# A two-layer decoder trunk in split fp32 on one core: the down projection in rounds of six, six, six and four hidden tiles, and the token factors stored as (rounded, rest) columns side by side

## The chip, the cores and the metric

The kernel runs on one core of a Trainium2 chip. The metric is device time of one execution in microseconds, as the median of three runs.

## The reference, cut to what matters

512 tokens of width 1024 go through a gated short convolution layer with a SwiGLU feed-forward stage, and then through a sliding-window attention layer with another one. All is float32. The change touches the two feed-forward stages alone:

```python
D_MODEL, SEQ = 1024, 512
D_FF = 2816

def swiglu(h, w_gate_up, w_down):
    g, u = jnp.split(h @ w_gate_up, 2, axis=-1)
    return (jax.nn.silu(g) * u) @ w_down

for l in range(2):
    ...  # conv or attention, with residual
    ff = swiglu(rmsnorm(h, ffn_pre_norm[l]), ffn_w_gate_up[l], ffn_w_down[l])
    h = h + rmsnorm(ff, ffn_post_norm[l])
```

## The kernel before

**Numbers.** Every float32 operand is split into a rounded part (`hi`, type fp32r) and the rest (`lo = x - hi`). A product is three TensorE matmuls, rounded by rest, rounded by rounded and rest by rounded (`mm3`, L191 to L193). ScalarE makes `hi` with a copy (L469 for the weights), VectorE subtracts for `lo` (L470).

**Hidden tiles.** The hidden width 2816 is 22 tiles of 128. The first two (`PLAIN`) are computed plainly. The other 20 go in ten *pairs*, q = 0 to 9. A pair's gate and up products are one 2 by 2 block matrix product, done with seven block products in place of eight: p = 1, 2, 6, 5, 7, 3, 4 in this order, one *job* each (`gate_jobs`). Products 1, 6, 7, 4 accumulate in one chain of PSUM banks, X (tile `gx`), products 5 and 3 in Z (`gz`), product 2 in Y (`gy`).

**Token factors.** Products 4 to 7 need sums and differences of token blocks. `factors()` makes them once per layer, in eight tiles `xt` of 128 by 1024. Such a tile holds two blocks of 256 columns: first the rounded columns of both, then the rests of both. For the products 6, 7 and 4 one matmul reads rounded and rest together as its moving operand (L1048, `two[:, :, c : c + 256]`, 2 by 256 columns, 512 apart in the tile) into 512 columns of PSUM, and a second multiplies the weight's rest with the 256 rounded columns (L1050). A pair has 3 x 8 such twos, a layer 240, the kernel 480.

**Down rounds.** The down projection is done in rounds over the hidden tiles that are ready, `ROUNDS`, again with seven block products, whose sum ends in SBUF tiles `mix`: after each product VectorE adds its two PSUM banks to `mix` (L639; in a layer's first round ScalarE makes eight of the fourteen by a copy, L637). A round of four tiles has 7 jobs with 1024 columns of weights each. A round of six has 11 (`order` in `down_jobs`): three hold the last third of two products, and there the next product of a chain follows its predecessor after six matmuls of another chain, and not after twelve. The last four hidden tiles have no such round: they are multiplied plainly in `close`, with four *closing* weights.

**The line.** All jobs of a layer stand in one line (`in_line`). With G for a pair's seven jobs and D for a down round's, the line is

```
G0 G1 G2 D0 G3 G4 D1 G5 G6 D2 G7 G8 G9 D3
```

Weights are fetched on SyncE's queue (L440) into seven buffers `raw`, split three jobs ahead of their use (`LINE_LEAD`), and used by TensorE. When a pair is done, the parts of making the down round's activations (`pair_sums`) are spread, one behind each job that follows; the first five jobs of an 11-job round take none (`alone`). The closing weights' splits stand in the line at `LAST`, 9, 7, 5 and 3 jobs from its end.

**Sums of weights in DRAM.** The block products need sums of weight blocks. They are made by GpSimd's DMA queue in DRAM (tiles `hsum`, L538), as plain copies and then accumulating transfers, in two or four steps (`Sums`). `BEGIN` says at which point of the program a block's steps begin: `0p1` is the end of pair 1 in layer 0, `0s1` the end of down round 1, `a3` a stage of the attention; `g09` are the sums for pair 9 of layer 0, `d02` for its down round 2. Each later point issues the next step, paced behind the splits.

Of the kernel before, what the change touches and what calls it, by code (L numbers as in the profile page):

```python
# [18 lines left out]
S = 512  # L19
KT = D // P  # L20
F = 2816
NF = F // P
ROUNDS = [(0, 6), (6, 10), (10, 14), (14, 18), (18, 22)]

PLAIN = 2

# [1 line left out]

BEGIN = {
# [4 lines left out]
}  # L34


# [36 lines left out]
def yoco_kernel(  # L73
# [45 lines left out]
    def wide(s, dt=F32):  # L119
        return wides.tile([P, D], dt, tag="wide", name=name(s))  # L120
# [118 lines left out]
    class Update:  # L239
# [124 lines left out]
        def factors(self):  # L364


            x = self.x[0]
            made = {p: [] for p in range(1, 8)}
            for p, k0, c in ((1, 0, 0), (2, 4, 0), (3, 4, 256)):
                made[p] = [[a[:, c : c + 256] for a in x[k0 + k]] for k in range(4)]  # L370
            for j in range(2):
                q11, q21, q12, q22 = (self.parts[i, hf, j] for hf in range(2) for i in range(2))

                nc.vector.tensor_tensor(out=q11, in0=q11, in1=q12, op=ALU.subtract)
                nc.vector.tensor_tensor(out=q12, in0=q22, in1=q12, op=ALU.subtract)
                nc.vector.scalar_tensor_tensor(out=q22, in0=q22, scalar=-1.0, in1=q11,
                                               op0=ALU.mult, op1=ALU.subtract)
                nc.vector.scalar_tensor_tensor(out=q21, in0=q22, scalar=-1.0, in1=q21,
                                               op0=ALU.mult, op1=ALU.subtract)
                for p, q in ((6, q22), (5, q11), (7, q12), (4, q21)):  # L380
                    two = wide("xt", F32R)
                    hi, lo = two[:, :S], two[:, S:]
                    two = two.rearrange("p (i c) -> p i c", i=2)
                    nc.scalar.activation(hi, q, AF.Copy)
                    nc.vector.tensor_tensor(out=lo, in0=q, in1=hi.bitcast(F32),
                                            op=ALU.subtract)
                    made[p] += [[hi[:, c : c + 256], lo[:, c : c + 256], two[:, :, c : c + 256]]
                                for c in (0, 256)]
            return made

    class Ahead:
# [156 lines left out]
    for l in range(2):  # L548
        for q in range((NF - PLAIN) // 2):
            sums_of[f"g{l}{q}"] = Sums([w_gb[l, q, b] for b in (2, 3, 0, 1)], [P, D],  # L550
                                        q not in ADDED)
        for rd, (f0, f1) in enumerate(ROUNDS[:-1]):
            k = slice(f0 // 2, f1 // 2)
# [401 lines left out]
    def ffn(l, before, ahead, gain, gpres, following):  # L955
# [5 lines left out]
        def gate_pair(pg, pu):  # L961
# [12 lines left out]
            return pair_sums(gr, acts[0])  # L974

        def gate_jobs(q, factors, out, to, then):


# [130 lines left out]

        acts = [[] for _ in ROUNDS]  # L1110
        mix = [None] * NB
        pss = [bank("pgu", ps_mm) for _ in range(4)]
        with tc.manual_schedule(engines=ALL):
# [29 lines left out]
            jobs, behind_one = [], []  # L1143
            for rd, (f0, f1) in enumerate(ROUNDS):
                last = rd == len(ROUNDS) - 1
                for f in range(max(f0, PLAIN), f1, 2):
                    q = (f - PLAIN) // 2
                    jobs += gate_jobs(q, factors, pair_acts if last else pair_sums, acts[rd],
                                      lambda q=q: sum_on(f"{l}p{q}"))
                    if behind_one and not (last and f < f1 - 2):  # L1150
                        jobs += behind_one.pop()
                if last:
                    break
                down = down_jobs(range(f0 // 2, f1 // 2), acts[rd], rd == 0,
                                 sums_of[f"d{l}{rd}"],
                                 lambda rd=rd: sum_on(f"{l}s{rd}"))
                behind_one.append(down)
# [260 lines left out]
    with tc.manual_schedule(engines=ALL):  # L1418
        last_tile(res, [[(0, 4)], [(0, 5)], [], [(0, 6), (0, 7), (1, 0), (1, 1)],
                        [(1, f) for f in (4, 5, 2, 3, 6, 7)]])  # L1420
        for hf in range(2):
            c = slice(hf * 256, (hf + 1) * 256)
# [194 lines left out]
```

## Time and profile before

| | |
|---|---|
| runs | 1026.5, 1026.7, 1026.81 us; median 1026.7 |
| the profiled execution | 1026.46 us, of which the span of instructions 1024.7 us |
| granted TensorE clock | 0.999 |
| DMA | 244.52 MB, mean 239 GB/s |

The profile is of one execution. "Busy" TensorE time is drawn with modelled ends: a matmul's row lasts longer than the distance to the next one's start, since they overlap. Where durations and starts differ, the starts tell the rate. Layer 0's feed-forward stage lies at about 188 to 500 us of the span, layer 1's at 693 to 1018 us.

### The profile page before, as it was taken

The page shows a single profiled execution, that of the slowest core. Times are in us where ns is not written, and L with a number is a line of the kernel's source. Part 1 is how long each engine was busy: PE and PEld are TensorE (multiplying, and loading weights), DVE is VectorE, ACT ScalarE, POOL GpSimd, SP SyncE. Part 2 cuts the span into 40 slices and gives each one's busy share as a digit, 9 for nine tenths or more (in the row PEclk, how much of TensorE's full clock was granted, in tenths as well). Part 3 has the DMA queues.
Part 4 walks back from the last instruction along what each step waited for, and adds up shares of the span by engine and source line. Part 5 has one row for each costly group of instructions (what it writes and reads, how often), then busy time and mean ns, then how long its engine had stood idle before and what let it go on. Part 6 is the DMA issues. An engine that isn't in the chain of part 4 may idle for free.

```text
span 1024.7 us, 16538 instructions
## 1 busy us (share of the span) xinstructions
PE 1015.1 (99%) x6168; PEld 900.3 (88%) x6168; DVE 858.7 (84%) x1440; ACT 582.3 (57%) x1035; POOL 196.9 (19%) x259
## 2 busy tenths in 40 slices
PE   9999999999999999999999999999999999999997
PEld 8888888999889898998897888889998998989986
DVE  5766767889789988989869998778997898889896
ACT  7323445865655454666476776677666554645641
POOL 0443033112111111000123653232111010110001
PEclk9999999999999999999999999999999999999999
DMA  9897689459979699879504779976899576998742
GB/s 357 288 266 225 184 255 350 136 167 292 348 238 296 195 305 307 267 210 318 170 5 160 187 229 277 254 264 153 270 289 328 167 245 226 299 298 249 240 149 82
DMA packets 66576, 244.52 MB, mean 239 GB/s; under 512 B 7872, under 2 KB 8384, under 8 KB 54720
## 3 DMA queue, kind: packets, MB, share of 16 engines
q1 hardware_dynamic: 51328, 145.98, 38.9%
q0 software_dynamic: 14592, 96.48, 36.9%
q8 instruction: 48, 0.79, 0.3%
q10 hardware_dynamic: 576, 1.02, 0.3%
q14 instruction: 32, 0.26, 0.1%
HBM read 237.15 MB, written 102.76 MB: 332 GB/s over the span
## 4 chain that ended last, share of the span: by engine, by line
PE 85%; DVE 8%; ACT 2%; DMA 2%; issue 2%; POOL 0%; DVEq 0%; ACTq 0%
PE gx L1048 10%; PE gx L1050 5%; PE pcub L191 4%; PE pcub L192 4%; PE pcub L193 4%; PE gz L193 3%; PE gz L192 3%; PE gz L191 3%; PE px L191 3%; PE px L193 3%; PE px L192 3%; PE pmix L191 2%; PE pmix L192 2%; PE pmix L193 2%; DMA raw<-in_w_gb_dram 2%; PE gy L193 2%
## 5 line engine op out<-in xcount | busy, mean ns | idle before, releaser
L470 DVE TENSOR_TENSOR wlo<-raw,whi 128x1024 fp32r<-128x1024 f32 x225 | 274.8, 1227 | 64.5 <-ACT whi L469 64.1
L469 ACT ACTIVATE whi<-raw 128x1024 fp32r<-128x1024 f32 x225 | 234.0, 1051 | 104.8 <-DVE raw L457 22.3
L1048 PE MATMUL gx<-xt,whi 128*128 128x512 f32 x480 | 172.5, 399 | 0.1
L1050 PE MATMUL gx<-xt,wlo 128*128 128x256 f32 x480 | 135.0, 281 | 0.0
L1048 PEld LDWEIGHTS gx<-xt,whi 128*128 128x128 f32 x480 | 90.4, 188 | 19.7 <-DVE st L1008 0.3
L538 POOL DMA_DIRECT2D hsum<-in_w_gb_dram x96 | 63.7, 751 | 143.9 <-ACT whi L469 82.6
L1050 PEld LDWEIGHTS gx<-xt,wlo 128*128 128x128 f32 x480 | 90.9, 189 | 0.1
L1024 ACT ACTIVATE st<-gx 128x256 f32<-128x256 f32 x120 | 43.0, 379 | 63.1 <-PE gx L1050 47.8
L538 POOL DMA_DIRECT2D hsum<-hsum x32 | 25.3, 790 | 258.9 <-ACT whi L469 192.0
L1008 DVE TENSOR_TENSOR st<-gx,st 128x256 f32<-128x256 f32 x160 | 62.9, 420 | 4.3 <-ACT st L1024 2.9
L192 PE MATMUL pcub<-xhi,whi 128*128 128x512 f32 x168 | 65.4, 389 | 0.0
L191 PE MATMUL pcub<-xlo,whi 128*128 128x512 f32 x168 | 65.4, 389 | 0.0
L193 PE MATMUL pcub<-xhi,wlo 128*128 128x512 f32 x168 | 65.4, 389 | 0.0
L1062 ACT ACTIVATE gr<-gr 128x1024 f32<-128x1024 f32 x20 | 21.3, 1065 | 49.2 <-DVE gr L1008 49.2
L191 PE MATMUL px<-wlo,ahi 128*128 128x512 f32 x120 | 46.8, 390 | 0.1
L192 PE MATMUL px<-whi,ahi 128*128 128x512 f32 x120 | 46.7, 389 | 0.0
L193 PE MATMUL px<-whi,alo 128*128 128x512 f32 x120 | 46.7, 389 | 0.0
L193 PE MATMUL gz<-xhi,wlo 128*128 128x256 f32 x160 | 45.4, 284 | 0.0
L191 PE MATMUL gy<-xlo,whi 128*128 128x256 f32 x160 | 45.3, 283 | 0.0
L192 PE MATMUL gy<-xhi,whi 128*128 128x256 f32 x160 | 45.3, 283 | 0.0
L193 PE MATMUL gy<-xhi,wlo 128*128 128x256 f32 x160 | 45.3, 283 | 0.0
L192 PE MATMUL gx<-xhi,whi 128*128 128x256 f32 x160 | 45.3, 283 | 0.0
(265 smaller groups left out, 3064.5 us busy)
## 6 DMA issues: line engine op xcount, KB each, us to landing
hsum<-in_w_gb_dram POOLq DMA_DIRECT2D x96, 512.0 KB, 7.9
raw<-hsum SPq DMA_DIRECT2D x88, 512.0 KB, 7.6
raw<-in_w_gb_dram SPq DMA_DIRECT2D x60, 512.0 KB, 7.6
hsum<-in_w_dn_dram POOLq DMA_DIRECT2D x36, 512.0 KB, 8.8
raw<-in_w_dn_dram SPq DMA_DIRECT2D x32, 512.0 KB, 6.0
hsum<-hsum POOLq DMA_DIRECT2D x28, 512.0 KB, 5.9
raw<-in_w_in_dram SPq DMA_DIRECT2D x21, 512.0 KB, 7.8
hsum<-in_w_dn_dram POOLq DMA_DIRECT2D x12, 768.0 KB, 12.8
```

The lines of the kernel that those rows point to most:

```text
L191: nc.tensor.matmul(out, whi, xlo, start=start, stop=False, **kw)
L192: nc.tensor.matmul(out, whi, xhi, start=False, stop=False, **kw)
L193: nc.tensor.matmul(out, wlo, xhi, start=False, stop=stop, **kw)
L469: self.begun = nc.scalar.activation(hi[:, :n], raw, AF.Copy)
L470: nc.vector.tensor_tensor(out=lo[:, :n], in0=raw, in1=hi[:, :n].bitcast(F32), op=ALU.subtract)
L538: nc.gpsimd.dma_start(dst, src, max_dma_last_dim=4 * 4 * S, **kw))
L1008: nc.vector.tensor_tensor(out=out, in0=a, in1=b, op=ALU.add)
L1024: nc.scalar.activation(ste, a, AF.Copy)
L1048: nc.tensor.matmul(banks[c][e], whi[:, kk], xboth[0], start=False, stop=False, **kw)
L1050: nc.tensor.matmul(banks[c][e][:, :256], wlo[:, kk], xhi, start=False, stop=k == 3 and p == 4, **kw)
L1062: nc.scalar.activation(kept[2], kept[2], AF.Silu)
```

## The change

Three edits. `ROUNDS` has four entries in place of five, so a layer has three down rounds, all of 11 jobs, and the line is

```
G0 G1 G2 D0 G3 G4 G5 D1 G6 G7 G8 G9 D2
```

`BEGIN` loses round 3's sums (`d03`, `d13`). Round 2's sums begin at the end of pair 4 in place of pair 1, and the sums for pair 9 at the end of pair 1 in place of round 1. In `factors()` a tile `xt` holds, for each of the two blocks, 256 rounded columns and then their 256 rests; L1048's moving operand is then 512 adjacent columns. ScalarE and VectorE write these halves with a step.

```diff
-ROUNDS = [(0, 6), (6, 10), (10, 14), (14, 18), (18, 22)]
+ROUNDS = [(0, 6), (6, 12), (12, 18), (18, 22)]
...
-    "0f1": "g05", "0p0": "g06", "0p1": "d02", "0p2": "g07", "0p3": "g08", "0s1": "g09", "0p5": "d03",
+    "0f1": "g05", "0p0": "g06", "0p1": "g09", "0p2": "g07", "0p3": "g08", "0p4": "d02",
...
-    "1f0": "g15", "1f1": "g16", "1p0": "d12", "1p2": "g17", "1p3": "g18", "1s1": "g19", "1p5": "d13",
+    "1f0": "g15", "1f1": "g16", "1p0": "g19", "1p2": "g17", "1p3": "g18", "1p4": "d12",
...
                     two = wide("xt", F32R)
-                    hi, lo = two[:, :S], two[:, S:]
-                    two = two.rearrange("p (i c) -> p i c", i=2)
+                    hi, lo = (two.rearrange("p (k i c) -> p k i c", k=2, i=2)[:, :, i]
+                              for i in range(2))
+                    q = q.rearrange("p (k c) -> p k c", k=2)
                     nc.scalar.activation(hi, q, AF.Copy)
                     nc.vector.tensor_tensor(out=lo, in0=q, in1=hi.bitcast(F32),
                                             op=ALU.subtract)
-                    made[p] += [[hi[:, c : c + 256], lo[:, c : c + 256], two[:, :, c : c + 256]]
-                                for c in (0, 256)]
+                    made[p] += [[two[:, c : c + 256], two[:, c + 256 : c + S],
+                                 two[:, c : c + S]] for c in (0, S)]
```

Three places show what moves. The first is GpSimd's queue of DRAM sums after pair 1 of layer 0; `hsum_146` to `149` are the sums for pair 6, `168` to `171` those of down round 2, of 512 KB. Before:

```order
L538 DMA hsum_146<-in_w_gb_dram 64x2048
L538 DMA hsum_147<-in_w_gb_dram 64x2048
L538 DMA hsum_168<-in_w_dn_dram 64x2048
L538 DMA hsum_169<-in_w_dn_dram 64x2048
L538 DMA hsum_170<-in_w_dn_dram 64x2048
L538 DMA hsum_171<-in_w_dn_dram 64x2048
L538 DMA hsum_148<-hsum_146 64x2048
```

Now, with `hsum_156` to `159` for pair 9 (lines are one higher in the changed file):

```order
L539 DMA hsum_146<-in_w_gb_dram 64x2048
L539 DMA hsum_147<-in_w_gb_dram 64x2048
L539 DMA hsum_156<-in_w_gb_dram 64x2048
L539 DMA hsum_157<-in_w_gb_dram 64x2048
L539 DMA hsum_158<-in_w_gb_dram 64x2048
L539 DMA hsum_159<-in_w_gb_dram 64x2048
L539 DMA hsum_148<-hsum_146 64x2048
```

At this place four transfers were exchanged for four of the same size. Round 2's own are 96x2048 (768 KB) now and stand three pairs later.

The second is VectorE at the start of layer 0's second down round, D1. `wlo` is a weight's rest, `px` and `pz` are the round's PSUM chains X and Z. Before, with 7 jobs:

```order
L639 TENSOR_TENSOR mix_2785<-mix_2785,px_3431 128x512
L639 TENSOR_TENSOR mix_2787<-mix_2787,px_3432 128x512
L470 TENSOR_TENSOR wlo_3448<-raw_3287,whi_3447 128x1024
L639 TENSOR_TENSOR mix_2795<-mix_2795,pz_3454 128x512
L639 TENSOR_TENSOR mix_2797<-mix_2797,pz_3455 128x512
```

Now, with 11 jobs:

```order
L471 TENSOR_TENSOR wlo_3679<-raw_3518,whi_3678 128x1024
L471 TENSOR_TENSOR wlo_3700<-raw_3520,whi_3699 128x1024
L640 TENSOR_TENSOR mix_2777<-mix_2777,px_3664 128x512
L640 TENSOR_TENSOR mix_2779<-mix_2779,px_3665 128x512
L640 TENSOR_TENSOR mix_2787<-mix_2787,pz_3685 128x512
L640 TENSOR_TENSOR mix_2789<-mix_2789,pz_3686 128x512
L471 TENSOR_TENSOR wlo_3723<-raw_3522,whi_3722 128x1024
```

The four additions of two products stand together, with no split between them, and a layer has three such places in each of D1 and D2.

The third is VectorE at the start of the last down round of layer 0, where the splits of the closing weights (L181) stand. Before (D3):

```order
L470 TENSOR_TENSOR wlo_4902<-raw_4715,whi_4901 128x1024
L1076 TENSOR_TENSOR alo_4908<-gr_4682,ahi_4907 128x512
L1076 TENSOR_TENSOR alo_4912<-gr_4682,ahi_4911 128x512
L181 TENSOR_TENSOR wlo_4917<-raw_4747,whi_4915 128x512
L181 TENSOR_TENSOR wlo_4918<-raw_4747,whi_4916 128x512
L639 TENSOR_TENSOR mix_2785<-mix_2785,px_4923 128x512
```

Now (D2):

```order
L181 TENSOR_TENSOR wlo_4798<-raw_4577,whi_4796 128x512
L181 TENSOR_TENSOR wlo_4799<-raw_4577,whi_4797 128x512
L1077 TENSOR_TENSOR alo_4807<-gr_4589,ahi_4806 128x512
L1077 TENSOR_TENSOR alo_4811<-gr_4589,ahi_4810 128x512
L471 TENSOR_TENSOR wlo_4829<-raw_4622,whi_4828 128x1024
L471 TENSOR_TENSOR wlo_4849<-raw_4655,whi_4848 128x1024
```

Before, two closing weights are split within G9, the third (`wlo_4917`) at its end and the fourth within D3. Now the first (`wlo_4798`) is split at the end of G9 and the other three within D2.

## The prediction

> **What bounds the kernel now.** I read the page's busy times first, then the groups of instructions by shape, then the timeline of single instructions.
>
> ```profile
> span 1024.7 us, 16538 instructions
> PE 1015.1 (99%) x6168; PEld 900.3 (88%) x6168; DVE 858.7 (84%) x1440; ACT 582.3 (57%) x1035; POOL 196.9 (19%) x259
> ```
>
> TensorE is busy for 99% of the span, so the kernel gets faster only where a matmul gets shorter, or where one of the few waits goes. The change leaves the matmuls' number and columns as they are (down: 3+2+2+2 = 9 pairs of hidden tiles a layer before, 3+3+3 = 9 now). What differs is the access of one group. The groups, by shape (count, busy us, mean ns of one):
>
> ```profile
> L1048 PE MATMUL gx<-xt,whi 128*128 128x512 f32 x480 | 172.5, 399 | 0.1
> L1050 PE MATMUL gx<-xt,wlo 128*128 128x256 f32 x480 | 135.0, 281 | 0.0
> L192 PE MATMUL pcub<-xhi,whi 128*128 128x512 f32 x168 | 65.4, 389 | 0.0
> L192 PE MATMUL gx<-xhi,whi 128*128 128x256 f32 x160 | 45.3, 283 | 0.0
> ```
>
> L1048 is the only group that reads its moving operand in two runs, and the only large one of 512 columns at 399 ns; the others read one run and stand at 389. These durations overlap, so I take the rate from starts (start us, duration, engine, line). One product of pair 1 with eight L1048/L1050 twos, then 24 matmuls of 256 columns:
>
> ```profile
> 241.12 0.40 PE L1048 MATMUL gx<-xt,whi 128*128 128x512 f32 x1
> ...
> 243.95 0.28 PE L191 MATMUL gx<-xlo,whi 128*128 128x256 f32 x1
> ...
> 246.82 0.28 PE L191 MATMUL gy<-xlo,whi 128*128 128x256 f32 x1
> ```
>
> and twelve matmuls of 512 columns read in one run, in a down round:
>
> ```profile
> 394.29 0.39 PE L191 MATMUL pz<-wlo,ahi 128*128 128x512 f32 x1
> ...
> 397.01 0.39 PE L191 MATMUL px<-wlo,ahi 128*128 128x512 f32 x1
> ```
>
> A two takes (243.95 - 241.12) / 8 = 353.8 ns. A one-run 256 takes (246.82 - 243.95) / 24 = 119.6 ns, a one-run 512 (397.01 - 394.29) / 12 = 226.7 ns, together 346.3.
>
> **Term 1, the moving operand in one run.** If L1048 comes to cost what other 512-column matmuls cost, a two gets 353.8 - 346.3 = 7.5 ns shorter, 480 x 7.5 = **3.6 us**. Bounds: nothing, if the excess belongs to the alternation of 512 and 256 columns and not to the two runs; 480 x (399 - 389) = 4.8 us by the mean durations. I take 3.6, since starts are what adds up. The gate jobs stay TensorE's: it is busy in all of them, and a pair of about 20 us gets 24 x 7.5 ns = 0.18 us shorter.
>
> [...]
>
> **Writing the factors.** `factors()` now writes in two runs on ScalarE and VectorE, sixteen times each. VectorE has two-run writes already, L1008's additions into `gr` (2 by 256), beside one-run ones into `mix`:
>
> ```profile
> L1008 DVE TENSOR_TENSOR gr<-gy,st 128x512 f32<-128x512 f32 x20 | 13.8, 689 | 0.6 <-PE gy L193 0.6
> L639 DVE TENSOR_TENSOR mix<-mix,px 128x512 f32<-128x512 f32 x54 | 35.2, 685 | 3.1 <-PE px L193 3.1
> ```
>
> 689 against 685 ns: 16 x 4 ns, nothing, and covered by the plain pairs' matmuls, which don't read the factors. Without that cover it would be 0.1 us.
>
> **Term 2, a down round less.** A round ends in fourteen additions to `mix`, whatever its length. Two layers lose a round each: 28 x 0.685 = 19.2 us of VectorE. None of it is on TensorE, so its worth is the waits that VectorE's lateness makes. These lie in four of the 10 us windows of the feed-forward stages (columns: window, length, busy us and count of PE, PEld, DVE, ACT, POOL, granted clock, DMA share, GB/s):
>
> ```profile
> 420.00:430.00 10.00, 9.86 (x70) 9.04 (x69) 9.90 (x18) 6.05 (x8) 0.00 (x0) 1.00 1.00 323
> 470.00:480.00 10.00, 9.97 (x46) 8.06 (x45) 9.70 (x15) 9.03 (x14) 0.00 (x0) 1.00 0.99 357
> 970.00:980.00 10.00, 9.97 (x60) 8.59 (x59) 9.63 (x16) 6.17 (x11) 0.00 (x0) 1.00 0.93 328
> 990.00:1000.00 10.00, 9.93 (x44) 8.10 (x44) 8.18 (x12) 0.73 (x2) 0.00 (x0) 1.00 0.01 2
> ```
>
> That is 0.14 + 0.03 + 0.03 + 0.07 = 0.27 us, but the drawn ends hide part of each wait. In the first one
>
> ```profile
> 421.94 0.28 PE L193 MATMUL gz<-xt,wlo 128*128 128x256 f32 x1
> 422.36 0.50 PE L1048 MATMUL gx<-xt,whi 128*128 128x512 f32 x1
> ```
>
> the starts are 0.42 us apart where 0.12 is the rule: 0.30 lost, 0.14 seen. Three of the four windows are the last pair and the last down round, with VectorE full: there the closing weights' splits come on top of a 7-job round. In the changed kernel three of the four closing weights are split within 11 jobs with 28.6 us of matmuls (21 x 6 of 226.7 ns), so these waits should go. Bounds: 0 (they only move) and 0.27 x 5 = 1.4 us (each longer wait hides up to 0.16 us, and so do shorter ones that are not seen). I take **0.8 us**.
>
> **Term 3, DMA.** The bytes stay. GpSimd issues 16 transfers less (two rounds of 8), SyncE 14 more, since a job with two products' rests has two fetches of 256 KB (a row: line, queue, count, KB, us to landing):
>
> ```profile
> hsum<-in_w_dn_dram POOLq DMA_DIRECT2D x36, 512.0 KB, 8.8
> hsum<-in_w_dn_dram POOLq DMA_DIRECT2D x12, 768.0 KB, 12.8
> raw<-hsum SPq DMA_DIRECT2D x88, 512.0 KB, 7.6
> raw<-hsum SPq DMA_DIRECT2D x8, 256.0 KB, 7.9
> ```
>
> After pair 1 the exchange is one for one (four transfers of 512 KB, then two). Round 2's sums begin during pair 5 and end during pair 7; D2 follows two pairs, some 40 us, later. So they are in time, and I take 0. What D1 sees is new: it follows pair 5 with 768 KB sums in flight. D0 does the same now after pair 2, with 512 KB ones. The bound from below is a loss, the second rival.
>
> **Where a wait could be added.** In an 11-job round the addition of X's banks must be done six matmuls after the product, which D0 shows now:
>
> ```profile
> 286.60 1.37 DVE L639 TENSOR_TENSOR mix<-mix,px 128x512 f32<-128x512 f32 x2 [0.69 <-PE px L193]
> ```
> ```profile
> 286.85 0.39 PE L193 MATMUL px<-whi,alo 128*128 128x512 f32 x1
> ...
> 288.44 0.39 PE L191 MATMUL px<-wlo,ahi 128*128 128x512 f32 x1
> ```
>
> VectorE had waited 0.69 us for the product, the first bank was read by 286.60 + 0.68 = 287.28, and TensorE came back to it at 288.44, with 1.16 us to spare. D1 and D2 make these additions on VectorE throughout, but the first falls into the third job, after two jobs (5.4 us of matmuls) with a split of 1.2 us each, so VectorE should wait there as in D0. Queued behind an addition are the next splits, three jobs ahead of TensorE. I take 0.
>
> **The sum.** The profiled execution took 1026.46 us, 1.8 of it outside the span, and lies 0.24 below the median. Against it 1026.46 - 3.6 - 0.8 = 1022.1; against the median **1022.3 us**.
>
> **Rivals.** *First: the excess is not the two runs'.* It would then be the alternation of widths. For it: no row shows 512 and 256 columns alternating in one run. Against it: a change of width where a down round meets a gate
>
> ```profile
> 410.38 0.39 PE L193 MATMUL px<-whi,alo 128*128 128x512 f32 x1
> ...
> 410.61 0.28 PE L191 MATMUL gx<-xlo,whi 128*128 128x256 f32 x1
> ```
>
> takes 0.23 us, no more than a 512 among its like. [...] Then only term 2 is left: 1025.9 us.
>
> *Second: weights come late in D1.* The wait at 421.94 had its beginning in a burst of sums before D2:
>
> ```profile
> 408.26 1.06 ACT L469 ACTIVATE whi<-raw 128x1024 fp32r<-128x1024 f32 x1 [4.55 <-DMA raw<-in_w_gb_dram]
> 409.35 1.23 DVE L470 TENSOR_TENSOR wlo<-raw,whi 128x1024 fp32r<-128x1024 f32 x1 [3.19 <-ACT whi L469]
> ...
> 410.84 0.28 PE L193 MATMUL gx<-xhi,wlo 128*128 128x256 f32 x1
> ```
>
> The rest was ready at 410.58 and used at 410.84. A 768 KB sum lands 12.8 - 8.8 = 4.0 us later than one of 512; if a weight behind it in D1 comes 4.0 us later at such a place, 4.0 - 0.26 = 3.7 us are lost: 1022.3 + 3.7 = 1026.0 in one layer, 1024.2 if half of it. Against it: D0 follows pair 2 and as many sums, and TensorE doesn't wait there, at a full DMA:
>
> ```profile
> 280.00:290.00 10.00, 10.00 (x45) 8.27 (x45) 9.28 (x15) 5.45 (x8) 0.00 (x0) 1.00 1.00 397
> ```
>
>
> *Third, the other side: the additions are late at every short distance.* The last round of layer 0 shows VectorE late:
>
> ```profile
> 473.88 0.39 PE L193 MATMUL px<-whi,a 128*128 128x512 f32 x1
> ```
> ```profile
> 476.93 1.28 DVE L639 TENSOR_TENSOR mix<-mix,px 128x512 f32<-128x512 f32 x2
> ```
>
> X's product had ended at 473.88 + 0.39 = 474.27, and the addition came 2.7 us later, behind splits. With 1.16 us to spare, such a lateness would cost 1.5 us at each of the twelve new places (three a round, D1 and D2, two layers): 1022.3 + 18 = 1040 us. It decides (slower than 1028.7) from 6.4 / 12 = 0.53 us each, a lateness of 1.7 us. Against it: that lateness came from closing splits in a 7-job round, and an 11-job round has 14 additions over 28.6 us and not over 19.
>
> **How the numbers follow.** 0.2% of 1026.7 is 2.05 us, about what a measurement of this kernel tells from no change: faster is below 1024.65, slower above 1028.75. The forecast has 0.66, the first rival 0.13 (no change), the second 0.14 (half of it faster, half no change), the third 0.05 (slower); 0.02 for a slowdown that I have not named. So faster 0.73, no change 0.20, slower 0.07. The range goes from term 1 and 2 at their upper bounds (1026.7 - 4.8 - 0.8 = 1021.1) to the first two rivals, 1026.0.
>
> **What would show it.** L1048's row falls from 399 to about 389 ns and eight twos take 2.77 us where 2.83 stand now; L1050's stays near 283. L639 has 74 rows where 102 stand (28 fewer), DVE some 18 us less busy. The windows of the last pair and round show no PE idle. The first rival: L1048 stays at 399. The second: ACT waits for DMA of several us within D1 (about 350 to 380 us and the like in layer 1) and PE below 9.9 there. The third: L639 additions starting over 1.2 us after the product in D1 and D2, with PE waits at the next `px`. Forecast and trace part if L1048 falls and the span doesn't: then a wait has taken its place, and the windows tell where.

## The result, and the profile after

The changed kernel is slower: 1034.21 us (median of 5 runs, 1033.53 to 1035.25) against 1026.68 us before (5 runs, 1026.09 to 1026.81), a ratio of 1.0077 with a 95% interval of 1.0066 to 1.0088. The forecast was 1022.3 us in a range up to 1026.0. The profiled execution took 1033.91 us, with a span of 1032.1, 7.4 us more than before.

The page's busy times and three rows of its groups, and then VectorE's additions from the groups by shape:

```profile
span 1032.1 us, 16515 instructions
PE 1016.6 (98%) x6168; PEld 901.7 (87%) x6168; DVE 843.8 (82%) x1414; ACT 583.7 (57%) x1037; POOL 186.2 (18%) x243
...
L470 ACT ACTIVATE whi<-raw 128x1024 fp32r<-128x1024 f32 x227 | 234.1, 1043 | 100.4 <-DMA raw<-hsum 24.3
L1049 PE MATMUL gx<-xt,whi 128*128 128x512 f32 x480 | 172.4, 399 | 0.0
...
L191 PE MATMUL px<-wlo,ahi 128*128 128x512 f32 x120 | 47.7, 398 | 6.7 <-DVE mix L640 6.7
```
```profile
L640 DVE TENSOR_TENSOR mix<-mix,px 128x512 f32<-128x512 f32 x38 | 25.3, 684 | 9.0 <-PE px L193 8.8
...
L640 DVE TENSOR_TENSOR mix<-mix,pz 128x512 f32<-128x512 f32 x22 | 14.6, 684 | 5.0 <-PE pz L193 5.0
...
L640 DVE TENSOR_TENSOR mix<-mix,py 128x512 f32<-128x512 f32 x14 | 9.3, 684 | 0.2 <-PE py L193 0.2
```

VectorE does 28 additions fewer (38 + 22 + 14 = 74), as forecast, and is 15 us less busy where 18 were forecast. But the 512-column matmul of a two stands at 399 ns as before, and 6.7 us of idle TensorE time now stand before matmuls into chain X, released by the addition to `mix`.

The 10 us windows tell where (us, busy us and count of PE, PEld, DVE, ACT, POOL, granted clock, DMA share, GB/s):

```profile
360.00:370.00 10.00, 8.86 (x39) 7.01 (x38) 8.76 (x11) 4.88 (x6) 1.80 (x3) 1.00 1.06 298
370.00:380.00 10.00, 8.85 (x40) 6.99 (x38) 6.02 (x11) 3.75 (x5) 0.00 (x0) 1.00 1.02 324
380.00:390.00 10.00, 9.22 (x47) 7.99 (x48) 9.11 (x13) 3.25 (x7) 0.00 (x0) 0.83 0.76 257
420.00:430.00 10.00, 10.00 (x76) 9.48 (x75) 9.90 (x16) 6.53 (x12) 0.00 (x0) 1.00 0.74 260
470.00:480.00 10.00, 10.00 (x45) 8.26 (x45) 10.00 (x14) 8.22 (x12) 0.00 (x0) 1.00 0.84 310
...
870.00:880.00 10.00, 8.30 (x37) 6.74 (x37) 8.75 (x11) 4.55 (x5) 1.59 (x2) 1.00 1.07 283
880.00:890.00 10.00, 8.48 (x38) 6.70 (x36) 6.06 (x11) 4.16 (x6) 0.00 (x0) 1.00 1.00 337
...
990.00:1000.00 10.00, 10.00 (x46) 8.28 (x45) 9.12 (x12) 2.73 (x3) 0.00 (x0) 1.00 0.02 8
```

The old waits at 420, 470 and 990 are gone: PE is full there. The new ones lie in D1, the second down round, of both layers, with the DMA queues full, and the second one of layer 0 is followed by a lower TensorE clock. By starts of matmuls (a distance less the usual 0.227 us) they are 1.30 us at 360.71, 2.09 at 378.46, 1.86 at 869.75 and 2.05 at 888.10, together 7.3 us. Behind each of them the next start is late by another 0.11 us (the first matmul's row lasts 0.50 and not 0.39), together 0.4. The lower clock adds 1.6. That is 9.3 us; without them the span would be 1022.8.

The second wait of layer 0 in single instructions: ScalarE, VectorE and TensorE.

```profile
368.01 1.06 ACT L470 ACTIVATE whi<-raw 128x1024 fp32r<-128x1024 f32 x1 [1.66 <-PE pz L193]
368.98 0.40 ACT L581 ACTIVATE a<-gr 128x256 fp32r<-128x256 f32 x1
375.74 1.58 ACT L470 ACTIVATE whi<-raw 128x1024 fp32r<-128x1024 f32 x2 [6.37 <-DMA raw<-hsum]
```
```profile
376.84 1.23 DVE L471 TENSOR_TENSOR wlo<-raw,whi 128x1024 fp32r<-128x1024 f32 x1 [3.94 <-ACT whi L470]
...
378.77 0.69 DVE L471 TENSOR_TENSOR wlo<-raw,whi 128x512 fp32r<-128x512 f32 x1
...
380.05 1.28 DVE L640 TENSOR_TENSOR mix<-mix,px 128x512 f32<-128x512 f32 x2
```
```profile
377.11 0.39 PE L193 MATMUL px<-whi,alo 128*128 128x512 f32 x1
...
378.46 0.39 PE L193 MATMUL py<-whi,alo 128*128 128x512 f32 x1
380.78 0.50 PE L191 MATMUL px<-wlo,ahi 128*128 128x512 f32 x1 [1.93 <-DVE mix L640]
```

Read from the top: ScalarE waits 6.37 us for a raw weight; VectorE's split waits for ScalarE; the X product ends at 377.11 + 0.39 = 377.50, and its addition, queued behind splits and small sums, comes 2.55 us later, at 380.05. TensorE is back at chain X after six matmuls and stands.

### The profile page after: what moved, and what is told of

Read it like the earlier page. It is cut to its first block, busy times and chain, and to the rows that moved or that the text cites. A ratio compares the mean times of both kernels' runs of the same rounds, so it can differ in the third digit from the quotient of the medians.

```text
span 1032.1 us, 16515 instructions
## 1 busy us (share of the span) xinstructions
PE 1016.6 (98%) x6168; PEld 901.7 (87%) x6168; DVE 843.8 (82%) x1414; ACT 583.7 (57%) x1037; POOL 186.2 (18%) x243
## 4 chain that ended last, share of the span: by engine, by line
PE 87%; DVE 6%; DMA 5%; ACT 1%; issue 1%; DVEq 0%; ACTq 0%
PE gx L1049 10%; PE gx L1051 5%; PE pcub L193 4%; PE pcub L191 4%; PE pcub L192 4%; PE gz L192 3%; PE gz L193 3%; PE gz L191 3%; DMA raw<-in_w_gb_dram 3%; PE px L191 3%; PE px L192 3%; PE px L193 3%; PE pmix L192 3%; PE pmix L193 3%; PE pmix L191 3%; PE gy L193 2%
## 5 line engine op out<-in xcount | busy, mean ns | idle before, releaser
L539 POOL DMA_DIRECT2D hsum<-hsum x28 | 22.3, 797 | 245.3 <-ACT whi L470 208.1
L297 POOL TENSOR_TENSOR ur<-uv,mhalf 128x1 f32<-128x1 f32 x15 | 13.8, 922 | 217.0 <-DVE uv L293 216.8
L192 PE MATMUL gz<-xt,whi 128*128 128x256 f32 x160 | 45.3, 283 | 0.0
```

What stands on the lines that cost most here:

```text
L192: nc.tensor.matmul(out, whi, xhi, start=False, stop=False, **kw)
L297: nc.gpsimd.tensor_tensor(out=self.r[:, t : t + 1], in0=self.v[:, t : t + 1], in1=mhalf[:, :1], op=ALU.pow)
L539: nc.gpsimd.dma_start(dst, src, max_dma_last_dim=4 * 4 * S, **kw))
```

## The experiments

Each is against its own runs of the kernel before, on the same chip. The first four take the change apart.

**The layout alone** (`factors()` as changed, `ROUNDS` and `BEGIN` as before).

> The kernel before with the new layout of the token factors alone; rounds and sums as before. Theory (the excess of a two belongs to the alternation of 512 and 256 columns, not to the hop in the moving operand): no change, 1026.7 us within 0.5, the one-run 512s still at 399 ns by mean duration, eight twos still in 2.83 us. Rival (the forecast's term 1, with the changed kernel's loss hiding the gain): 1023.1 us.

Measured: 1026.19 us against 1026.27, ratio 0.9997 (0.9988 to 1.0006). From its groups by shape:

```profile
L1049 PE MATMUL gx<-xt,whi 128*128 128x512 f32 x480 | 172.4, 399 | 0.0
```

The operand is one run of 512 columns now, and the mean duration is still the 399 ns that it was with the operand in two runs. The layout is worth nothing here.

**The rounds and sums alone** (as changed, with the old layout).

> The changed kernel with the old layout of the factors: rounds and sums as changed. Theory (the whole loss comes from the rounds and the sums' places): 1034.2 us within 1, with the same two waits of TensorE for an addition of chain X in the second down round of each layer. Rival (the layout does cost something, for instance by its two-run writes): below 1032.

Measured: 1034.75 us, ratio 1.0074 (1.0060 to 1.0088). The loss is all there. The waits are not those of the changed kernel's profile: D1's are 0.49 and 2.11 us in layer 0, 2.44 and 0.49 in layer 1, and a fifth, 1.98, stood in D0 of layer 0, which the profiled execution of the changed kernel did not have. So D0 is at its margin too. The three long ones are each followed by the lower clock.

**The third round's sums at the end of D1.**

```diff
-... "0p3": "g08", "0p4": "d02",
+... "0p3": "g08", "0s1": "d02",
...
-... "1p3": "g18", "1p4": "d12",
+... "1p3": "g18", "1s1": "d12",
```

> The changed kernel with the third round's sums begun at the end of the second down round (both layers) instead of the end of the fourth and fourteenth pair, so that no 768 KB sum is on its way during pair 5 and the second down round. Theory (the sums' burst makes weights late in the second round, and these hold up the additions): the four waits go or fall below 0.3 us each, which takes away about 9 us: 1025 to 1026.5 us. Rival (the second round is late whatever the DMA does, since additions stand behind splits in VectorE's queue): 1032 or more, with the four waits in place.

Measured: 1025.67 us, ratio 0.9988 (0.9979 to 0.9997). The windows:

```profile
280.00:290.00 10.00, 8.61 (x39) 6.83 (x37) 6.63 (x12) 5.52 (x8) 0.00 (x0) 1.00 0.99 394
...
360.00:370.00 10.00, 10.00 (x45) 8.26 (x44) 7.86 (x11) 4.33 (x5) 0.00 (x0) 1.00 0.89 289
370.00:380.00 10.00, 10.00 (x46) 8.28 (x45) 9.21 (x15) 4.41 (x6) 0.00 (x0) 1.00 0.56 183
...
870.00:880.00 10.00, 10.00 (x46) 8.26 (x44) 8.56 (x13) 3.32 (x5) 0.00 (x0) 1.00 0.65 213
```

All four waits are gone, with additions, rounds and layout as in the changed kernel. Each against its own runs of the kernel before, a loss of 7.5 us has become a gain of 0.6. One wait, 1.55 us, stands in D0 (280 to 290).

**The additions ahead of a split.** In a job with two products' rests the split of the weight two jobs on is made between the products and not ahead of both; weights and sums are as in the changed kernel.

```diff
                     for p, c in parts:
+                        if at and job.between:
+                            job.between()
                         product(p, cs[c], *(w[:, at : at + S * len(cs[c])] for w in job.w))
...
-            prepare(j + LINE_LEAD)
-            if paced and j + LINE_LEAD < len(jobs):
-                issue(1 + len(issues) // 6, jobs[j + LINE_LEAD].begun)
+            def splits(n=j + LINE_LEAD):
+                prepare(n)
+                if paced and n < len(jobs):
+                    issue(1 + len(issues) // 6, jobs[n].begun)
+
+            if j + 1 < len(jobs) and jobs[j + 1].mid:
+                jobs[j + 1].between = splits
+            else:
+                splits()
```

> The changed kernel, sums where it has them, but in the jobs with two products' rests the split of the weight two jobs ahead is put behind the first product's additions on VectorE instead of ahead of them. Weights come as late as in the changed kernel. Theory (a late weight alone would be hidden; TensorE waits only because chain X's additions are queued behind its split): the four waits shrink to below 0.5 us each and the time is 1025 to 1027.5 us, while ScalarE still waits several us for DMA in the second rounds. Rival (the weight itself is too late): TensorE waits for the split in place of the addition, 1031 us or more.

Measured: 1033.37 us, ratio 1.0063 (1.0050 to 1.0076). The first waits of both D1 are gone, the second ones grew to 2.34 and 2.79 us, each with the lower clock behind it. VectorE there:

```profile
376.04 1.23 DVE L472 TENSOR_TENSOR wlo<-raw,whi 128x1024 fp32r<-128x1024 f32 x1 [1.60 <-ACT whi L471]
377.18 0.42 DVE L592 TENSOR_TENSOR s<-gr 128x256 f32<-128x256 f32 x1
...
378.31 0.42 DVE L593 SCALAR_TENSOR_TENSOR s<-s,gr 128x256 f32<-128x256 f32 x1
378.65 1.28 DVE L647 TENSOR_TENSOR mix<-mix,px 128x512 f32<-128x512 f32 x2
```

TensorE was ready for the next job at 377.04. Its own weight was complete at 376.04 + 1.23 = 377.27, so late by 0.2 us; then came four small sums (1.4 us) that the late weight had pushed along, and only then the addition. So the first wait belongs to the order on VectorE, and the second to a weight so late that one place in the queue doesn't help. The theory holds for one of two, and the time is the rival's. An order with the additions ahead of the small sums as well was not tried.

**Plain copies for the accumulating transfers** of the third round's sums. The kernel leaves these additions out, so its output is not the reference's.

```diff
+            if rd == 2:
+                sums = sums_of[f"d{l}{rd}"]
+                sums.steps = [[(dst, src, None) for dst, src, op in step]
+                              for step in sums.steps]
```

> The changed kernel in which the accumulating transfers of the third round's sums (in both layers, four a layer of 768 KB) are plain copies of the same size: these sums are left out, so the output isn't the reference's. The same transfers stand at the same places of GpSimd's queue; they only take less time of the DMA queues (a plain packet of 8 KB takes 309 ns, an accumulating one 628). Theory (the second rounds wait for DMA time, of which the accumulating transfers take twice the plain ones'): the second wait of each round (2.05 to 2.09 us) falls by half or more, the first by less; 1027 to 1031 us. Rival (the number of transfers or their order on the queue decides): no change, 1034 us.

Measured: 1030.61 us (1028.03 to 1034.02), ratio 1.0046 (1.0032 to 1.0059). In the profiled execution the second waits are gone and the first are as they were, 1.29 and 1.99 us. It was the fastest of the six, 1028.03 us; the others took 0.9 to 6 us more, two of them with a granted clock of 0.995 and 0.996, where the kernel before has 0.998 to 0.999. So second waits may have stood in them. The profiled execution's windows in D1:

```profile
360.00:370.00 10.00, 8.87 (x39) 7.02 (x38) 8.24 (x10) 3.72 (x5) 1.04 (x2) 1.00 1.05 365
370.00:380.00 10.00, 10.00 (x45) 8.26 (x44) 9.30 (x16) 5.47 (x7) 0.00 (x0) 1.00 0.99 389
```

The DMA queues say why. Both views are of the 15 us from 359 to 374 (queue, packets, MB, share of the 16 engines' time; q0 is GpSimd's, q1 SyncE's with the weights). First the changed kernel, then this one:

```profile
q0 software_dynamic: 264, 1.90, 60.9%
q1 hardware_dynamic: 1246, 2.46, 44.3%
```
```profile
q1 hardware_dynamic: 1543, 3.44, 61.1%
q0 software_dynamic: 304, 2.10, 41.8%
```

With accumulating sums a MB on GpSimd's queue takes 0.609 x 15 / 1.90 = 4.8 us of all engines; here, with one accumulating transfer left among plain ones, 3.0; a MB of weights takes 2.7 in both. In the same traces a packet of 8 KB on GpSimd's queue takes 628 ns where it accumulates and 309 where it is plain. In this full stretch the accumulating sums take the time that the weights need: 2.46 MB of weights arrive in place of 3.44.

**The two together**, plain copies and the additions first.

> The changed kernel with two of the earlier edits together: the third round's accumulating transfers are plain copies (these sums are left out, so the output isn't the reference's), and a first product's additions stand ahead of the split two jobs on. Theory (the first wait of a second round belongs to the order on VectorE, the second to DMA time, and these are all): no wait over 0.5 us in the second rounds and 1024 to 1026 us. Rival (a late weight shows elsewhere once both are gone): 1028 us or more.

Measured: 1025.41 us, ratio 0.9990 (0.9981 to 0.9999). One wait of 0.28 us is left, in layer 1. These sums, too, are left out. So D1's loss is these two parts.

**The two kinds of sums exchanged.** The third round's (768 KB) at the changed kernel's places of the last pair's (512 KB), and the other way round.

> The changed kernel with the third round's sums (768 KB each) and the last pair's sums (512 KB each) exchanged in their places: the 768 KB ones begin one pair ahead of the first round, the 512 KB ones one pair ahead of the second. Theory (what counts is how much the sums in flight load the DMA queues at the round that follows): the second rounds' waits fall to 1 to 3 us in all, the first round of layer 0 gets a wait of 2 us or more, with the clock's drop behind it; 1029 to 1033 us. Rival (the second round is the sensitive one, whatever the size): the waits stay, 1034 us or more.

Measured: 1034.22 us, ratio 1.0077 (1.0063 to 1.0091). By its time the rival had it, by its trace the theory:

```profile
270.00:280.00 10.00, 9.23 (x41) 7.30 (x41) 5.95 (x5) 6.91 (x9) 3.46 (x5) 1.00 1.07 337
280.00:290.00 10.00, 10.00 (x46) 8.23 (x44) 2.84 (x4) 2.45 (x4) 0.00 (x0) 1.00 1.00 274
290.00:300.00 10.00, 5.28 (x14) 3.90 (x13) 8.87 (x14) 4.73 (x6) 0.00 (x0) 0.70 0.88 357
...
360.00:370.00 10.00, 10.00 (x48) 8.38 (x47) 9.75 (x14) 5.62 (x7) 2.36 (x3) 1.00 1.05 363
370.00:380.00 10.00, 10.00 (x46) 8.29 (x45) 8.07 (x10) 4.56 (x5) 0.00 (x0) 1.00 1.01 291
```

D1 has no wait at all. D0 of layer 0 has them, one of 0.93 and one of 4.88 us with 2.8 us of lower clock behind, and D0 of layer 1 one of 1.05. The loss went with the 768 KB sums; that the two times agree is chance.

**The 512s ahead of the 256s** (the kernel before, one loop made two).

```diff
-                        for k in range(4):
+                        twos = c == "X" and len(factors[p][0]) > 2
+                        for k in range(4) if twos else ():
+                            kk = slice(e * S + k * P, e * S + (k + 1) * P)
+                            nc.tensor.matmul(banks[c][e], whi[:, kk], factors[p][k][2],
+                                             start=False, stop=False, **kw)
+                        for k in range(4):
```

> The kernel before, old layout, with one change of order: in the products 6, 7 and 4 of a pair the four matmuls of 512 columns are issued first and the four of 256 columns after them, not in turn. Theory (the 7.5 ns that a two takes beyond its parts come from the turn between the widths and not from the hop): eight twos take 2.77 to 2.79 us instead of 2.83 and the time falls by 3 to 3.6 us, to 1022.7 to 1023.5 us. Rival (each 512 of this group is slow by itself, whatever stands beside it): no change, 1026.3 us.

Measured: 1025.57 us, ratio 0.9992 (0.9983 to 1.0000). Eight twos:

```profile
241.45 1.09 PE L1047 MATMUL gx<-xt,whi 128*128 128x512 f32 x4
...
244.26 0.28 PE L191 MATMUL gx<-xlo,whi 128*128 128x256 f32 x1
```

(244.26 - 241.45) / 8 = 351.3 ns against 353.8 in this one product. Starts are read to 10 ns, so the medians over all 60 products of the trace tell more: 350.9 against 354.0. That is 3.1 ns, 480 x 3.1 = 1.5 us, where the medians of the runs differ by 0.9 (the interval reaches to no change). So some four tenths of the excess, now 354.0 - 346.3 = 7.7 ns, belong to the turn between widths, and the theory's 3 to 3.6 us did not come. Within the groups the 512s still start 224 to 236 ns apart.

**Another tile under the 512s.**

> The kernel before with the new layout, in which the 512-column matmuls of the products 6, 7 and 4 read another tile of 512 columns, the rounded columns of the normed tokens, which ScalarE wrote in one run; the rounded-and-rest operand of these products is left out, so the output isn't the reference's. What is still open: grouping took away 1.2 us of 3.6, so some 5 ns of a two belong neither to the hop nor to the turn of widths. Theory (they belong to the tile that is read): the 512s start 227 to 231 ns before the next matmul instead of 236, 2 to 3 us less, 1023.5 to 1024.5 us. Rival (they belong to the place, the weights or the PSUM banks): no change, 1026.3 us.

Measured: 1026.11 us, ratio 0.9998 (0.9989 to 1.0006), 399 ns as before. The tile that is read is not it. Whether the weights or the PSUM banks are was not tried: some 5 ns of a two stay unexplained.

**Versions to beat both.** Three edits on the changed kernel: sums after D1, additions first, 512s first.

> The changed kernel with three edits together: the third round's sums begin at the end of the second round, the additions of a first product stand ahead of the split two jobs on, and the 512s of a product are issued ahead of its 256s. Theory (the parts add: 8.5 us from the sums' place, 0 to 1.5 from the additions, which may take away the wait left in the first round, 3 to 3.6 from the grouping if that works): 1020.5 to 1023 us. Without a gain from the grouping 1024 to 1026.

Measured: 1023.69 us, ratio 0.9974 (0.9964 to 0.9984), between the two ranges that were expected. Then besides these the last pair's sums from the end of D0 (`"0s0": "g09"`, `"1s0": "g19"`):

> As the kernel with three edits together, and besides the last pair's sums begin at the end of the first round (in both layers) and not ahead of it, so that no block's sums begin in the pair ahead of a down round except the pair's own neighbours. Theory: the wait of 1.5 us in the first round of layer 0 goes for good and nothing comes in its place: 1019.5 to 1022 us. Rival (the sums crowd the middle pairs, so that a wait appears there or in the second round): 1024 us or more.

Measured: 1023.23 us, ratio 0.9968 (0.9955 to 0.9980); no wait in any down round, and still 1.2 us above the expected range. The same without the edit of the additions:

> The kernel with the sums spread, the 512s ahead of the 256s and the additions first, without the last of the three: additions stand behind the splits as in the changed kernel. Theory (with the sums out of the way the weights are in time, and the order on VectorE costs nothing): 1023.2 us within 0.8. Rival (the short distances cost something by themselves): 1024.5 us or more, with waits of TensorE for an addition of chain X.

Measured: 1023.10 us, ratio 0.9969 (0.9957 to 0.9981). This is as fast as the one before it, and simpler. Its windows in D0 and D1:

```profile
280.00:290.00 10.00, 10.00 (x46) 8.29 (x45) 9.28 (x15) 5.44 (x8) 0.00 (x0) 1.00 0.73 245
360.00:370.00 10.00, 10.00 (x46) 8.29 (x45) 8.07 (x10) 4.55 (x5) 0.00 (x0) 1.00 0.98 334
370.00:380.00 10.00, 10.00 (x46) 8.29 (x45) 9.21 (x15) 4.11 (x6) 0.00 (x0) 1.00 0.54 165
```

Where the weights are in time, as here, the short distances cost nothing: PE is busy for 10.00 of 10 us in all three windows.

## Why the prediction was wrong

**Term 1 (3.6 us) failed.** The step was "If L1048 comes to cost what other 512-column matmuls cost". The one group with a hop was the slow one, but not for the hop: the layout alone gave 0. The first rival, at 0.13, was right in that nothing was gained by the layout, and right in its cause for some four tenths of the excess; the rest stays open. The trace of the kernel before had a hint that the step passed over, since not all the others "stand at 389":

```profile
L191 PE MATMUL pq<-xlo,whi 128*128 128x512 f32 x64 | 26.6, 415 | 0.0
```

These 64 read one run of 512 columns and are slower than the group with the hop: those that stand behind narrower matmuls take 0.48 us, as at 585.44. One hop in 512 columns costs nothing that these runs show: 399 ns and 1026.27 us with it, 399 ns and 1026.19 us without.

**Term 2 (0.8 us) was right in its mechanism and too small.** The waits at 420, 470 and 990 went. By starts of matmuls all waits of the feed-forward stages before add up to 1.5 us, and none of them is left: the bound of 1.4 for waits hidden by drawn ends was a little too tight. And the term looked for them in those stages alone. Two more stood just behind layer 0's, at 510.84 and 524.36 us, where TensorE enters the attention and waits for outputs of ScalarE and VectorE, 0.8 us together. They are gone too: from the first of them to layer 1's first matmul into `pgu` it takes 173.7 us before (510.84 to 684.53), 173.6 with the layout alone, and 172.9 in the changed kernel (515.60 to 688.46). So the term is worth 2.3 us.

**"I take 0" for the sums failed, and with it the direction.** The step was the argument against the second rival: "D0 follows pair 2 and as many sums, and TensorE doesn't wait there". As many, but of 512 KB; with 768 KB in front of it D0 waits 0.93 and 4.88 us (the exchanged sums). The window quoted for D0 stood at a DMA share of 1.00: that was a sign that there was no room, and was read as a sign that a full DMA does no harm. The prediction counted the sums' bytes and issues, and not that an accumulating MB takes 1.8 times the DMA time of a MB of weights (4.8 us against 2.7).

**"I take 0" for the additions failed as its consequence.** "VectorE should wait there as in D0" holds only while the splits ahead of an addition have their weights. The second and the third rival were priced as if they were apart: a late weight at its own job (up to 3.7 us in one layer), and late additions at twelve places with the weights in time. What came is one feeding the other: a late weight holds its split, the split holds the addition behind it, and the addition is wanted six matmuls after its product, at the start of the next job, where the last of the splits ahead of it serves the job after that. In the profiled execution it came at four places of the twelve, the first and the third of D1's three in both layers, and cost 1.3 to 2.1 us at each. D2 had none. Taking away either part alone shows it: the plain copies remove the second waits (in the profiled execution), the order on VectorE the first, and both together all but 0.28 us.

**The sum, made again:** 0 for term 1, -2.3 for term 2, +7.3 for four waits, +0.4 for the late starts behind them, +1.6 for the clock, together +7.0. The spans differ by 7.4; of the remaining 0.4, 0.3 lies ahead of layer 0's first matmul into `pgu` (at 179.43 in place of 179.17). The clock's part was in no rival.

The signs that the prediction named for the second rival, waits of ScalarE for DMA between 350 and 380 us and PE below 9.9, are those that came; the one for the first rival, 399 ns, came too, and so did, in D1, the third's, additions over 1.2 us behind their product with a wait of TensorE at the next `px`.

## What to carry to other kernels

A full DMA queue in a quoted window is a warning: before moving or enlarging transfers, add up the DMA time by kind (accumulating ones apart: 4.8 us a MB here, beside 2.7 for weights) in the stretch where they land, and look which weights are fetched there. Where an in-order queue holds both a step that waits for a transfer and a step that the critical engine waits for soon, price the two risks together, since lateness of the first is charged at the need of the second. A slow group with one odd property may have two; change the property alone before its cost is put into a sum.

## What the runs showed of the hardware

In the changed kernel a wait of 2.09 us was followed by half of TensorE's clock for some 3.4 us. After the wait at 378.46:

```profile
381.91 0.63 PE L192 MATMUL px<-whi,ahi 128*128 128x512 f32 x1
382.33 0.63 PE L193 MATMUL px<-whi,alo 128*128 128x512 f32 x1
...
384.89 0.51 PE L193 MATMUL px<-whi,alo 128*128 128x512 f32 x1
385.24 0.39 PE L191 MATMUL px<-wlo,ahi 128*128 128x512 f32 x1
```

(384.89 - 381.91) / 7 = 0.426 us a matmul, where 0.227 is the rule, and a granted clock of 0.83 between 380 and 390 us is half the clock for 0.17 x 10 / 0.5 = 3.4 us. It cost about 1.6 us there, besides the 0.11 that stands behind each of the four waits of this execution. In the traces of the down rounds, waits of 0.28 to 1.99 us left the clock alone with one exception at 1.98; of those from 2.05 to 2.79 one (2.05) left it alone and five of 2.09, 2.11, 2.34, 2.44 and 2.79 did not; the 4.88 cost 2.8 us. The wait of 2.09 us was thus nearly doubled in price.

The traces' records of the clock suggest why 2 us is not a sharp limit: the slow stretches begin on a grid. The one in the changed kernel lasts 3.413 us (381.73 to 385.14). In the kernel with the rounds and sums alone they begin at 291.27, 383.43 and 874.95 us, and the distances, 92.16 and 491.52, are 27 and 144 times 3.413; the slow stretch behind the wait of 4.88 us lasts 6.83, twice that. If a wait counts by its part between two points of the grid, the 1.99 (parts of 0.69 and 1.30) falls among those without a drop, as it did. Only the 2.05 (1.99 within one stretch, no drop) and the 1.98 (all within one, a drop) are not told apart by this, so the limit, as an estimate from these waits, would lie at about 2 us of a stretch of 3.4.
